# Moving expert gathers and six value tiles into an earlier stage of a fused decoder block, with a one-matmul gate scatter

## The chip, the cores and the metric

The kernel runs on one NeuronCore of a Trainium2 chip. The metric is the device time of one execution in microseconds (us); lower is better. Engines are named PE (TensorE; PEld is its weight loads), DVE (VectorE), ACT (ScalarE), POOL (GpSimd) and SP (SyncE, which here only issues DMAs).

## The reference

One decoder layer on 256 tokens of width 1024, fp32. Two gated attention mixers feed a merge, and the second half is a product-key expert layer (PEER). Only that half is touched:

```python
def peer_ffn(h, w_q, sub_k1, sub_k2, expert_u, expert_v):
    q = (ht @ w_q).reshape(T, 8, 256)
    s1, s2 = q[..., :128] . sub_k1, q[..., 128:] . sub_k2      # 128 keys each
    v1, i1 = top_k(s1, 16);  v2, i2 = top_k(s2, 16)
    vals, pos = top_k(v1 + v2 over all 256 pairs, 16)          # per token and head
    experts = i1[...] * 128 + i2[...];  gates = softmax(vals)
    a = einsum('cd,chkd->chk', x, expert_u[experts])
    return einsum('chk,chkd->cd', gelu(a) * gates, expert_v[experts])
```

Each token has 8 heads x 16 = 128 experts out of 16,384, and an expert is one row of 1024 floats in `expert_u` and one in `expert_v`.

## The kernel before, in words

The first 289 us compute the mixers, the merge, the second norm and the queries. What follows is the expert layer, in three stages that this document calls R, U and V.

**Two ways to the same sum.** The last 160 tokens (`ND`) go through all 16,384 experts densely. For each of 128 u tiles (128 experts x 1024, 512 KB from HBM), `u_tile` (L585) does eight fp32 matmuls of 160 columns into a PSUM bank, applies gelu, and leaves the activations in `ga`. In stage V, each of 128 v tiles is multiplied with `ga` by eight more such matmuls into four accumulators `acc` (L855). The first 96 tokens (`NG`, as sets of 64 and 32) use gathers: 96 indirect DMAs fetch 128 rows of u each (512 KB) into a tile `grow`, DVE takes the dot products (L622); 96 more fetch rows of v, which DVE scales and adds into `accG` (L633).

**Stage R** (u tiles 0 to 59): beside the u tiles, DVE finds the experts of all tokens (`retrieval`), in four pieces. Each piece decodes positions to indices with bf16 one-hots (L715) that are multiplied with a table, fp32 before (L717). `route` transposes indices and gates on PE (`ps_tri`, L751) into `eTb` and `gT`. The exponentials of a piece are summed on DVE (`se`, L729) before `tri` and these transposes.

**Stage U** (u tiles 60 to 127): the gates have to be put into `ga`, a zero nearly everywhere. `gate_group` (L802) does it for four tokens at a time, 40 times: DVE builds the one-hots `o2` and `o1` of both index halves (L811, L812), ACT multiplies `o1` by the gate (`og`, L814), DVE by the gate's rounding remainder (L815), and PE multiplies the one-hots, two f16 matmuls of 128 columns a token (L819). DVE and ACT multiply the result into `ga`.

**Stage V** (v tiles 0 to 127): the matmuls of L855, the remaining gathers, and for each v tile a `mark`: DVE copies one column of the loaded tile (L857).

**What sets the order.** Tile loads are issued by SP in program order into nine buffers (three tags with three buffers each), so that load i waits for the readers of tile i-9: PE, and in V also the mark. Gathers are issued by POOL, two at a time after every second gather's use, into two buffers of two slots: gathers n+3 and n+4 are issued when gather n (odd) has been read. `gather_steps(rate)` (L642) puts the uses into the program: `STEPS_R`, `STEPS_U` and `STEPS_V` are gathers per tile in R, U and V. Every engine works strictly in its own program's order.

**The end.** After the last v tile the accumulators are copied to `accT`, PE folds `accG` over its partitions (L865) and transposes `accT` on top (L872), DVE adds the residual `x1` (L875), and four DMAs write the output.

```python
STEPS_R, STEPS_U, STEPS_V = 0.55, 0.8, 0.9
...
if n % 2 == 1:                     # after the use of gather n
    for m in (n + 3, n + 4):
        fetch(m)
```

Of the kernel before, what the change touches and what calls it, by code (L numbers as in the profile page):

```python
# [39 lines left out]
STEPS_R = 0.55  # L40
STEPS_U = 0.8
STEPS_V = 0.9
GT = 4
# [27 lines left out]
def block_kernel(ctx: ExitStack, tc, x, g2, consts, small, wqkv, wkv5, wmg, w1kv, wup, wout, wq, uT, u, v, folds, out):  # L71
# [487 lines left out]
    gTb = ep.tile([P, 2, S], F16, name="gTb")  # L559
# [91 lines left out]
    with ExitStack() as ts:  # L651
# [8 lines left out]
        def retrieval(h, hg, tri):  # L660
# [14 lines left out]
            idf = sp.tile([P, 2, QH, TOPK], F32, name="idf")  # L675
            nc.vector.tensor_copy(idf, idx)
# [30 lines left out]
            diff = sp.tile([P, QH, TOPK], F32, name="diff")  # L707
            nc.vector.tensor_copy(diff[:, :, 0:1], idf[:, 0, :, 0:1])
            nc.vector.tensor_sub(diff[:, :, 1:], idf[:, 0, :, 1:], idf[:, 0, :, :TOPK - 1])
            hs = slice(QH * hg, QH * hg + QH)  # L710
            for w, (pos, op, table) in enumerate(((pa, ALU.is_ge, diff), (pb, ALU.is_equal, idf[:, 1]))):
                posb = sp.tile([P, QH, TOPK], BF16, name="posb")
                nc.vector.tensor_copy(posb.rearrange("p h j -> p (h j)"), pos)
                oh = sp.tile([P, QH, TOPK, TOPK], BF16, name="oh", tag="oh")
                nc.vector.tensor_tensor(oh, posb.unsqueeze(2).to_broadcast([P, QH, TOPK, TOPK]),  # L715
                                        steps16[:, w].unsqueeze(1).to_broadcast([P, QH, TOPK, TOPK]), op=op)
                nc.vector.tensor_mul(oh, oh, table.unsqueeze(3).to_broadcast([P, QH, TOPK, TOPK]))  # L717
                o2 = sp.tile([P, QH, TOPK // 2, TOPK], BF16, name="oh2", tag="oh2")
# [28 lines left out]
        def route(h, tri):  # L747
            with tc.issue_after(state["pe"].ins):
                pt = bank("ps_tri", "g")[:, :3 * P].rearrange("p (i t) -> p i t", t=P)
                for i in range(3):  # L750
                    nc.tensor.transpose(pt[:, i, :], tri[:, i].rearrange("p h j -> p (h j)"), C("ident"))  # L751
            nc.vector.tensor_copy(eTb[:, :, h * P:(h + 1) * P], pt[:, 0:2])
            r = slice(h * P, (h + 1) * P)
            nc.vector.tensor_copy(gTb[:, 0, r], pt[:, 2])
            nc.vector.tensor_copy(gT[:, r], gTb[:, 0, r])
            nc.vector.tensor_sub(gTb[:, 1, r], pt[:, 2], gT[:, r])
# [73 lines left out]

    groups = ND // GT
    done = 0
    for i in range(TOPK_TILES, NKEY):
# [7 lines left out]
        gather_steps(STEPS_U)  # L841

# [26 lines left out]
    for j in range(2):
        for h in (1, 0):  # L870
            for c in range(4):
                nc.tensor.matmul(fin[h][j][:, c * P:(c + 1) * P], accT[:, 4 * j + c, h * P:(h + 1) * P], cident,  # L872
                                 start=h == 1 and c == 0, stop=c == 3, skip_group_check=True)
            o = x1[:, h, j * 512:(j + 1) * 512]
            nc.vector.tensor_add(o, fin[h][j], o)  # L875
            nc.sync.dma_start(out[h, :, j * 512:(j + 1) * 512], o)
# [113 lines left out]
```

## Time and profile before

| | us |
|---|---|
| median of 3 runs | 942.36 (941.22 to 951.69) |
| the profiled execution's own time | 938.46 |
| its span in the profile | 936.7 |
| PE busy | 900.6 (96%) |
| DVE busy | 614.3 (66%) |
| ACT busy | 309.6 (33%) |
| POOL busy | 218.4 (23%) |
| mean granted TensorE clock | 0.999 of full |

The span is the time from the first to the last instruction of the program; the execution's own time has the launch around it. Stage R lasts from 289.3 to 425.7 us, U from 425.7 to 611.2, V from 611.2 to 925.4, and the end to 936.7. A busy share is an average over stages with different limits, so it is read by stage. An fp32 matmul of the program is recorded as two matmuls in the trace, a bf16 or f16 one as one.

### The profile page before, as it was taken

To read this page: it belongs to the slowest core of one execution; us is meant where nothing else is said; L and a number is where in the kernel's file an instruction comes from. 1 tells how busy PE (TensorE), PEld (TensorE's weight loads), DVE (VectorE), ACT (ScalarE), POOL (GpSimd) and SP (SyncE) were. 2 spreads that over 40 slices of the span, in tenths; PEclk is the share of its full clock that TensorE was granted. 3 is DMA by queue.
4 is the path that set the end of the run, shared out by engine and by line. 5 is a ranking of instruction groups with operands and counts; after the bars stand their busy time and mean duration, and the time that the engine had idled before them with its cause. 6 is when DMAs were issued, how large, how long until landed. Compare 5 with 4: busy or idle time off the path is not lost.

```text
span 936.7 us, 17034 instructions
## 1 busy us (share of the span) xinstructions
PE 900.6 (96%) x6433; PEld 842.9 (90%) x6433; DVE 614.3 (66%) x1663; ACT 309.6 (33%) x768; POOL 218.4 (23%) x213
## 2 busy tenths in 40 slices
PE   8999999999999999999999999999989989998987
PEld 6778867998899999999999999999988888988986
DVE  5886876577567689997778788644445544444444
ACT  6766776545541221326555455300000000000000
POOL 2000000000100223233232233333344333443330
PEclk9999999999999999999999999999999999999999
DMA  7665401556556999999999999999999999999994
GB/s 242 191 213 190 159 1 47 183 185 210 169 173 235 331 392 365 376 373 328 350 334 352 354 339 347 354 378 403 357 369 399 400 380 403 385 392 401 400 398 185
DMA packets 79570, 281.96 MB, mean 301 GB/s; under 512 B 10176, under 2 KB 10432, under 8 KB 79488
## 3 DMA queue, kind: packets, MB, share of 16 engines
q1 hardware_dynamic: 51088, 177.63, 52.6%
q0 software_dynamic: 28400, 103.25, 29.2%
q8 instruction: 51, 0.84, 0.3%
q14 instruction: 31, 0.25, 0.1%
HBM read 278.64 MB, written 1.05 MB: 299 GB/s over the span
## 4 chain that ended last, share of the span: by engine, by line
PE 56%; DMA 28%; issue 7%; POOL 3%; DVE 3%; ACT 2%; DVEq 0%; POOLq 0%; ACTq 0%; SPq 0%
PE ps_u L588 28%; DMA grow<-in_v_dram,gidx 21%; PE ps_g L819 4%; POOL grow L611 3%; DMA grow<-in_u_dram,gidx 3%; PE ps_q L121 2%; PE ps_mg L124 2%; PE ps_mg L121 2%; PE ps_q L124 2%; PE ps_q L122 2%; PE ps_mg L122 2%; PE ps_s L410 2%; PE ps_proj L171 1%; PE ps_pt L427 1%; DVE wlo L106 1%
## 5 line engine op out<-in xcount | busy, mean ns | idle before, releaser
L855 PE MATMUL acc<-ga,uvraw 128*128 128x160 f32 x2048 | 292.9, 302 | 21.3 <-DMA uvraw<-in_v_dram 19.5
L855 PEld LDWEIGHTS acc<-ga,uvraw 128*128 128x128 f32 x2048 | 279.9, 190 | 34.2 <-DMA uvraw<-in_v_dram 32.3
L588 PE MATMUL ps_u<-h2f,uvraw 128*128 128x160 f32 x2048 | 287.3, 299 | 0.0
L588 PEld LDWEIGHTS ps_u<-h2f,uvraw 128*128 128x128 f32 x2048 | 280.7, 190 | 0.1
L633 DVE SCALAR_TENSOR_TENSOR accG<-grow,gwt,accG 128x1024 f32<-128x1024 f32 x94 | 120.8, 1285 | 137.0 <-DMA grow<-in_v_dram,gidx 136.9
L611 POOL DMA_INDIRECT grow<-in_u_dram,gidx x96 | 102.1, 1063 | 302.2 <-DVE gdot L622 149.1
L611 POOL DMA_INDIRECT grow<-in_v_dram,gidx x96 | 106.0, 1104 | 166.0 <-DVE mark L857 150.0
L622 DVE CUSTOM_DVE_ANT_0 grow<-grow,h2d 128x1024 f32<-128x1024 f32 x96 | 116.7, 1218 | 34.6 <-DMA grow<-in_u_dram,gidx 34.5
L106 DVE TENSOR_TENSOR wlo<-wraw,whi 128x1024 fp32r<-128x1024 f32 (+1 forms) x80 | 95.5, 1196 | 37.1 <-ACT whi L105 37.0
L105 ACT CAST whi<-wraw 128x1024 fp32r<-128x1024 f32 (+1 forms) x80 | 82.0, 1029 | 65.5 <-PE ps_q L122 13.9
L868 ACT COPY accT<-acc 128x320 f32<-128x320 f32 x2 | 0.9, 426 | 270.9 <-PE acc L855 270.9
L592 ACT ACTIVATE ga<-ps_u 128x160 f32<-128x160 f32 (+32 forms) x124 | 33.5, 271 | 143.7 <-PE ps_u L588 143.4
L814 ACT ACTIVATE og<-o,gT 128x128 f16<-128x128 f16 x160 | 61.9, 568 | 15.9 <-PE ps_g L819 14.5
L819 PE MATMUL ps_g<-og,o 128*128 128x128 f16 x320 | 44.4, 294 | 0.0
L819 PEld LDWEIGHTS <-o 128*128 128x128 f16 x320 | 36.3, 116 | 1.5
L168 PE MATMUL ps_proj<-whi,hhi 128*128 128x512 f32 (+1 forms) x96 | 36.3, 381 | 1.3 <-ACT hhi L205 1.0
L489 POOL DMA_DIRECT2D gain<-in_g_dram x1 | 0.5, 533 | 151.2 <-DVE wlo L106 151.2
L169 PE MATMUL ps_proj<-whi,hlo 128*128 128x512 f32 (+1 forms) x96 | 35.7, 378 | 0.0
L121 PE MATMUL ps_mg<-hhi,whi 128*128 128x256 f32 x128 | 32.3, 288 | 0.0
L596 DVE TENSOR_TENSOR ga<-ga,au 128x160 f32<-128x160 f32 (+32 forms) x68 | 16.8, 247 | 23.4 <-ACT au L595 22.9
L122 PE MATMUL ps_mg<-hlo,whi 128*128 128x256 f32 x128 | 31.9, 285 | 0.0
L121 PE MATMUL ps_q<-h2hi,whi 128*128 128x256 f32 x128 | 31.7, 285 | 0.2 <-ACT h2hi L105 0.2
(256 smaller groups left out, 1126.0 us busy)
## 6 DMA issues: line engine op xcount, KB each, us to landing
uvraw<-in_uT_dram SPq DMA_DIRECT2D x128, 512.0 KB, 6.8
uvraw<-in_v_dram SPq DMA_DIRECT2D x128, 512.0 KB, 7.2
wraw<-in_wqkv_dram SPq DMA_DIRECT2D x20, 512.0 KB, 4.7
wraw<-in_wmg_dram SPq DMA_DIRECT2D x16, 512.0 KB, 3.6
wraw<-in_wq_dram SPq DMA_DIRECT2D x16, 512.0 KB, 4.3
wraw<-in_w1kv_dram SPq DMA_DIRECT2D x8, 512.0 KB, 4.0
wraw<-in_wup_dram SPq DMA_DIRECT2D x8, 512.0 KB, 3.6
wraw<-in_wout_dram SPq DMA_DIRECT2D x8, 512.0 KB, 4.5
```

Source lines behind the costliest of these rows:

```text
L105: nc.scalar.copy(hi, src)
L106: state["dve"] = nc.vector.tensor_sub(lo, src, hi)
L121: nc.tensor.matmul(ps, lh, rh, start=i == 0, stop=False)
L122: nc.tensor.matmul(ps, ll if lo_last else lh, rh if lo_last else rl, start=False, stop=False)
L124: nc.tensor.matmul(ps, lh if lo_last else ll, rl if lo_last else rh, start=False, stop=i == NC - 1)
L588: state["pe"] = nc.tensor.matmul(ps, raw[:, c * P:(c + 1) * P], h2f[:, c, NG:], start=c == 0, stop=c == NC - 1)
L611: nc.gpsimd.indirect_dma_start(out=dst, out_offset=None, in_=src, in_offset=bass.IndirectOffsetOnAxis(ap=gidx[:, j:j + 1], axis=0))
L622: nc.vector.tensor_tensor_reduce(out=g, in0=g, in1=h2d[k], scale=1.0, scalar=0.0, op0=ALU.mult, op1=ALU.add, accum_out=gdot[:, j:j + 1])
L633: nc.vector.scalar_tensor_tensor(accG[:, k], g, gwt[:, j:j + 1], accG[:, k], op0=ALU.mult, op1=ALU.add)
L814: nc.scalar.activation(og[0][:, :, k], o1[:, :, k], AF.Copy, scale=gT[:, t0 + k:t0 + k + 1])
L819: nc.tensor.matmul(ps[:, k, :], o2[:, :, k], og[i][:, :, k], start=i == 0, stop=i == 1, skip_group_check=True)
L855: nc.tensor.matmul(acc[c // 2][:, c % 2, 0:ND], raw[:, c * P:(c + 1) * P], ga_at(i), start=i == 0 and c % 2 == 0, stop=i == NKEY - 1, skip ...
```

## The change

- The gate scatter takes one fp32 matmul a token in place of two f16 ones: `o2` and `og` become fp32, the remainder's DVE product and the split tables `gTb` go.
- The decode tables (`diff`, and the second half of the indices, `idb`) become bf16.
- `STEPS_R` goes from 0.55 to 0.6 and `STEPS_U` from 0.8 to 1.0; `STEPS_V` stays.
- Six v tiles are fetched in U into a pool of their own (`first_v`), one every eighth u tile.
- Each mark is put behind the DVE instruction that `state["dve"]` names.
- The last two v tiles are worked accumulator by accumulator (bank by bank), and each bank's fold, transposes, add and output DMA (256 columns of both halves) are done in turn, alternately from SP and ACT.

```diff
-STEPS_R = 0.55
-STEPS_U = 0.8
+STEPS_R = 0.6
+STEPS_U = 1.0
 STEPS_V = 0.9
+FIRST_V = 6
+LAST = 2
...
-    def load_raw(src, i):
-        raw = wp.tile([P, DM], F32, name="uvraw", tag=("wraw", "whi", "wlo")[i % 3])
-        nc.sync.dma_start(raw, src[i])
+    def load_raw(src, i, home=None):
+        tag = f"first{i}" if home else ("wraw", "whi", "wlo")[i % 3]
+        raw = (home or wp).tile([P, DM], F32, name="uvraw", tag=tag)
+        state["sp"] = nc.sync.dma_start(raw, src[i])
...
-            idf = sp.tile([P, 2, QH, TOPK], F32, name="idf")
-            nc.vector.tensor_copy(idf, idx)
+            idf = sp.tile([P, QH, TOPK], F32, name="idf")
+            nc.vector.tensor_copy(idf, idx[:, 0])
+            idb = sp.tile([P, QH, TOPK], BF16, name="idb")
+            nc.vector.tensor_copy(idb, idx[:, 1])
...
-            diff = sp.tile([P, QH, TOPK], F32, name="diff")
+            diff = sp.tile([P, QH, TOPK], BF16, name="diff")
...
-            nc.vector.tensor_copy(gTb[:, 0, r], pt[:, 2])
-            nc.vector.tensor_copy(gT[:, r], gTb[:, 0, r])
-            nc.vector.tensor_sub(gTb[:, 1, r], pt[:, 2], gT[:, r])
+            nc.vector.tensor_copy(gT[:, r], pt[:, 2])
...
-        o2 = op.tile([P, P, n], F16, name="o2")
+        o2 = op.tile([P, P, n], F32, name="o2")
         o1 = op.tile([P, P, n], F16, name="o1")
-        og = [op.tile([P, P, n], F16, name=f"og{i}") for i in range(2)]
+        og = op.tile([P, P, n], F32, name="og")
...
-            nc.scalar.activation(og[0][:, :, k], o1[:, :, k], AF.Copy, scale=gT[:, t0 + k:t0 + k + 1])
-        nc.vector.tensor_mul(og[1], o1, rows(gTb[:, 1]))
+            nc.scalar.activation(og[:, :, k], o1[:, :, k], AF.Copy, scale=gT[:, t0 + k:t0 + k + 1])
         ps = bank("ps_g", "g").rearrange("p (t i) -> p t i", i=P)
         for k in range(n):
-            for i in range(2):
-                nc.tensor.matmul(ps[:, k, :], o2[:, :, k], og[i][:, :, k], start=i == 0, stop=i == 1,
-                                 skip_group_check=True)
+            nc.tensor.matmul(ps[:, k, :], o2[:, :, k], og[:, :, k], start=True, stop=True, skip_group_check=True)
...
+    first_v = pool(ctx, "first_v", 1)
+    early = []
...
         gather_steps(STEPS_U)
+        if i % 8 == 0 and i >= TOPK_TILES + 8 and len(early) < FIRST_V:
+            with tc.issue_after(state["sp"].ins):
+                early.append(load_raw(v, len(early), first_v))
...
-        state["dve"] = nc.vector.tensor_copy(mark, raw[:, 0:1])
-        gather_steps(STEPS_V if i < NKEY - 4 else 2 * NG)
+        with tc.issue_after(state["dve"].ins):
+            state["dve"] = nc.vector.tensor_copy(mark, raw[:, 0:1])
+        gather_steps(STEPS_V if i < NKEY - 5 else 2 * NG)
...
+    def finish(q):
+        r = slice(q * 256, (q + 1) * 256)
         for k in range(len(SETS)):
+            nc.tensor.matmul(fin[q][:, 0], fold[:, k], accG[:, k, r], start=k == 0, stop=False, skip_group_check=True)
+        for h in range(NH):
+            for c in range(2):
+                nc.tensor.matmul(fin[q][:, h, c * P:(c + 1) * P], accT[:, 2 * q + c, h * P:(h + 1) * P], cident,
+                                 start=False, stop=c == 1, skip_group_check=True)
+        nc.vector.tensor_add(x1[:, :, r], fin[q], x1[:, :, r])
+        (nc.scalar if q % 2 else nc.sync).dma_start(outr[:, :, r], x1[:, :, r])
+
     for q in range(4):
+        for c in (2 * q, 2 * q + 1):
+            for i in range(LAST):
+                state["pe"] = nc.tensor.matmul(acc[q][:, c % 2, 0:ND], raws[i][:, c * P:(c + 1) * P],
+                                               ga_at(NKEY - LAST + i), start=False, stop=i == LAST - 1,
+                                               skip_group_check=True)
         (nc.scalar.copy if q % 2 else nc.vector.tensor_copy)(accT[:, 2 * q:2 * q + 2, NG:], acc[q][:, :, 0:ND])
+        if q:
+            with tc.issue_after(state["pe"].ins):
+                finish(q - 1)
+    finish(3)
```

How the change moves instructions, at two places on DVE (the number behind a name tells buffers apart). The first is the end of R, where the last piece's `se` and `tri` precede the transposes that open U; the `L622` and `L624` rows with `grow` are each the use of one gather. Before:

```order
L722 TENSOR_TENSOR tri_3068<-oh2_4648 128x64
L622 ISA grow_4481,gdot_2760<-grow_4481,h2d0_2514 128x1024
...
L622 ISA grow_4590,gdot_2760<-grow_4590,h2d0_2514 128x1024
...
L622 ISA grow_4590,gdot_2760<-grow_4590,h2d0_2514 128x1024
...
L729 TENSOR_REDUCE se_4684<-ex_4681 128x4
L730 RECIPROCAL se_4684<-se_4684 128x4
L731 SCALAR_TENSOR_TENSOR tri_3068<-ex_4681,se_4684 128x64
L752 CAST eTb_2752<-ps_tri_4713 128x2x128
```

and of the change:

```order
L726 TENSOR_TENSOR tri_3067<-oh2_4658 128x64
L624 ISA grow_4513,gdot_2759<-grow_4513,h2d0_2514 128x1024
...
L624 ISA grow_4600,gdot_2759<-grow_4600,h2d0_2514 128x1024
...
L624 ISA grow_4600,gdot_2759<-grow_4600,h2d0_2514 128x1024
...
L624 ISA grow_4664,gdot_2759<-grow_4664,h2d0_2514 128x1024
...
L733 TENSOR_REDUCE se_4694<-ex_4691 128x4
L734 RECIPROCAL se_4694<-se_4694 128x4
L735 SCALAR_TENSOR_TENSOR tri_3067<-ex_4691,se_4694 128x64
```

Before, three uses stood between the last index piece and `se`, the 26th to the 28th of all; now there are four, the 28th to the 31st. The 28th is the second of its buffer, the 31st the first of the buffer that is fetched when the 28th has been read.

The second is the turn from U to V (`ga<-ga,au` is a late u tile's product, `mark` belongs to a v tile). Before:

```order
L596 TENSOR_TENSOR ga_1_4741<-ga_1_4741,au_6674 128x152
L622 ISA grow_6524,gdot_2760<-grow_6524,h2d0_2514 128x1024
...
L826 SCALAR_TENSOR_TENSOR ga_0_2765<-ps_g_6692,ga_0_2765 128x60x4
L826 SCALAR_TENSOR_TENSOR ga_1_4741<-ps_g_6692,ga_1_4741 128x62x4
L857 COPY mark_6833<-uvraw_6834 128x1
L596 TENSOR_TENSOR ga_1_4741<-ga_1_4741,au_6716 128x156
L622 ISA grow_6620,gdot_2760<-grow_6620,h2d0_2514 128x1024
...
L857 COPY mark_6833<-uvraw_6836 128x1
L857 COPY mark_6833<-uvraw_6847 128x1
L596 TENSOR_TENSOR ga_1_4741<-ga_1_4741,au_6732 128x156
```

and of the change:

```order
L598 TENSOR_TENSOR ga_1_4750<-ga_1_4750,au_6640 128x160
L635 SCALAR_TENSOR_TENSOR accG_2760<-grow_6595,gwt_2758,accG_2760 128x1024
L866 COPY mark_6653<-uvraw_5125 128x1
L635 SCALAR_TENSOR_TENSOR accG_2760<-grow_6595,gwt_2758,accG_2760 128x1024
L866 COPY mark_6653<-uvraw_5354 128x1
L866 COPY mark_6653<-uvraw_5581 128x1
L635 SCALAR_TENSOR_TENSOR accG_2760<-grow_6628,gwt_2758,accG_2760 128x1024
L866 COPY mark_6653<-uvraw_5810 128x1
L866 COPY mark_6653<-uvraw_6037 128x1
```

Before, the first marks stood among U's last products, and 78 gather uses (of 192) came ahead of the first mark; now all of U's products come first, with 99 uses. The last use stands behind mark 122 before and behind mark 104 now, and 22 marks follow it without one. Up to the sixteenth mark there are 94 uses before and 110 now. Ahead of the first gate one-hot of U there are 28 before and 31 now. On SP, the six early v loads stand singly among the u loads, the last of them 14 u loads ahead of the other 122.

## Rows read from the trace of the kernel before

**Rows 1.** The page, part 4: the chain that ended last, by engine and line.

```profile
PE 56%; DMA 28%; issue 7%; POOL 3%; DVE 3%; ACT 2%; DVEq 0%; POOLq 0%; ACTq 0%; SPq 0%
```

**Rows 2.** Windows: stretch, us; PE, PEld, DVE, ACT, POOL busy; clock, DMA share, GB/s.

```profile
289.30:425.70 136.40, 136.40 (x1015) 136.31 (x1014) 115.40 (x536) 34.72 (x82) 34.33 (x32) 1.00 0.92 349
425.70:611.20 185.50, 185.50 (x1409) 183.98 (x1408) 140.43 (x379) 93.63 (x335) 54.67 (x52) 1.00 0.95 345
611.20:660.00 48.80, 48.80 (x362) 48.80 (x361) 21.92 (x48) 0.52 (x2) 18.50 (x18) 1.00 1.00 392
660.00:925.40 265.40, 244.07 (x1692) 231.17 (x1691) 128.97 (x204) 0.43 (x1) 101.29 (x92) 1.00 0.99 385
```

**Rows 3.** The chain in order of time: start us, us, what.

```profile
355.98 26.08 PE ps_u L588 x192
...
429.10 0.94 PE ps_g L819 x8
...
928.89 3.59 PE fin L872 x32
```

**Rows 4.** Waits of SP's queue in V: total us, times, longest.

```profile
SPq L582 <- DVE mark L857: 233.9, 95, 5.4
```

**Rows 5.** Waits of DVE for gathers, in V and in U.

```profile
DVE accG L633 <- DMA grow<-in_v_dram,gidx: 136.9, 93, 3.7
...
DVE grow L622 <- DMA grow<-in_u_dram,gidx: 10.1, 10, 1.9
```

**Rows 6.** The uses of v gathers: ns min/median/max, first and last start us.

```profile
L633 DVE SCALAR_TENSOR_TENSOR accG<-grow,gwt,accG x94: 1283/1285/1346, 657.7 to 922.6; 128x1024 f32<-128x1024 f32 x94
```

**Rows 7.** DMA issues, 430 to 600 us: what, count, median us to landing.

```profile
uvraw<-in_v_dram SPq DMA_DIRECT2D x4, 512.0 KB, 5.0
...
grow<-in_u_dram,gidx POOLq DMA_INDIRECT x50, 7.8
```

**Rows 8.** Timeline at the turn from R to U.

```profile
418.53 1.22 DVE L622 CUSTOM_DVE_ANT_0 grow<-grow,h2d 128x1024 f32<-128x1024 f32 x1
...
420.02 1.68 POOL L611 DMA_INDIRECT grow<-in_u_dram,gidx  x1 [8.10 <-DVE gdot L622]
...
421.96 0.21 DVE L729 TENSOR_REDUCE se<-ex 128x4 f32<-128x64 f32 x1
...
423.13 0.49 PE L751 MATMUL ps_tri<-cst,tri 128*128 128x128 f32 x3
```

**Rows 9.** Groups by form: busy us, mean ns, idle before.

```profile
L622 DVE CUSTOM_DVE_ANT_0 grow<-grow,h2d 128x1024 f32<-128x1024 f32 x96 | 116.7, 1218 | 34.6 <-DMA grow<-in_u_dram,gidx 34.5
...
L819 PEld LDWEIGHTS <-o 128*128 128x128 f16 x320 | 36.3, 116 | 1.5
...
L815 DVE TENSOR_TENSOR og<-o,gTb 128x512 f16<-128x512 f16 x40 | 16.7, 417 | 0.0
L811 DVE TENSOR_TENSOR o<-iob,eTb 128x512 f16<-128x512 f16 x40 | 16.6, 415 | 0.0
...
L715 DVE TENSOR_TENSOR oh<-posb,steps 128x1024 bf16<-128x1024 bf16 x8 | 5.5, 688 | 0.1
L717 DVE TENSOR_TENSOR oh<-oh,diff 128x1024 bf16<-128x1024 bf16 x4 | 4.9, 1225 | 0.0
...
L245 DVE TENSOR_TENSOR q_h<-q_h,sml 128x512 f32<-128x512 f32 x6 | 4.0, 684 | 0.0
L872 PEld LDWEIGHTS fin<-cident,accT 128*128 128x128 f32 x32 | 3.7, 192 | 0.5 <-issue 0.5
```

**Rows 10.** Eight stretches of 25 us in V: the slowest and the fastest.

```profile
750.00:775.00 25.00, 21.94 (x152) 20.56 (x151) 10.95 (x17) 0.00 (x0) 8.50 (x9) 1.00 0.99 375
...
850.00:875.00 25.00, 22.71 (x158) 21.66 (x159) 12.29 (x19) 0.00 (x0) 10.15 (x9) 1.00 1.02 405
```

**Rows 11.** Busy time by stretch: the last 2.2 us, behind the last matmul.

```profile
934.50:936.70 2.20, 0.00 (x0) 0.00 (x0) 0.00 (x0) 0.00 (x0) 0.00 (x0) 0.57 0.12 44
```

**Rows 12.** Timeline: the opening matmuls of the program.

```profile
1.24 3.59 PE L192 MATMUL ps_heat<-heat 128*128 128x512 bf16 x8 [1.24 <-DVE heat L189]
```

More of the change, by code (lines that the diff above doesn't have):

```diff
@@ L558, in block_kernel @@
     gT = ep.tile([P, S], F32, name="gT")
-    gTb = ep.tile([P, 2, S], F16, name="gTb")
     dp = pool(ctx, "dots", 2)
@@ L706, in retrieval @@
             yield 1.6
-            diff = sp.tile([P, QH, TOPK], F32, name="diff")
-            nc.vector.tensor_copy(diff[:, :, 0:1], idf[:, 0, :, 0:1])
-            nc.vector.tensor_sub(diff[:, :, 1:], idf[:, 0, :, 1:], idf[:, 0, :, :TOPK - 1])
+            diff = sp.tile([P, QH, TOPK], BF16, name="diff")
+            nc.vector.tensor_copy(diff[:, :, 0:1], idf[:, :, 0:1])
+            nc.vector.tensor_sub(diff[:, :, 1:], idf[:, :, 1:], idf[:, :, :TOPK - 1])
             hs = slice(QH * hg, QH * hg + QH)
-            for w, (pos, op, table) in enumerate(((pa, ALU.is_ge, diff), (pb, ALU.is_equal, idf[:, 1]))):
+            for w, (pos, op, table) in enumerate(((pa, ALU.is_ge, diff), (pb, ALU.is_equal, idb))):
                 posb = sp.tile([P, QH, TOPK], BF16, name="posb")
@@ L848, in block_kernel, with v_load @@
     mark = dp.tile([P, 1], F32, name="mark", bufs=1)
-    ahead = []
-    for i in range(NKEY):
+    ahead = early
+    def v_load(i):
         while len(ahead) <= AHEAD and i + len(ahead) < NKEY:
             ahead.append(load_raw(v, i + len(ahead)))
-        raw = ahead.pop(0)
+        return ahead.pop(0)
+    for i in range(NKEY - LAST):
+        raw = v_load(i)
         for c in range(NC):
             nc.tensor.matmul(acc[c // 2][:, c % 2, 0:ND], raw[:, c * P:(c + 1) * P], ga_at(i),
-                             start=i == 0 and c % 2 == 0, stop=i == NKEY - 1, skip_group_check=True)
-        state["dve"] = nc.vector.tensor_copy(mark, raw[:, 0:1])
-        gather_steps(STEPS_V if i < NKEY - 4 else 2 * NG)
+                             start=i == 0 and c % 2 == 0, stop=False, skip_group_check=True)
+        with tc.issue_after(state["dve"].ins):
+            state["dve"] = nc.vector.tensor_copy(mark, raw[:, 0:1])
+        gather_steps(STEPS_V if i < NKEY - 5 else 2 * NG)
     accT = hpool.tile([P, NC, S], F32, name="accT", tag="h2f")
@@ L861, in block_kernel @@
     psum.append(psd)
-    fin = [[bank("fin", "u", 3) for j in range(2)], [bank("fin", "u", 3), bank("fin1", "g")]]
-    for j in range(2):
-        for k in range(len(SETS)):
-            nc.tensor.matmul(fin[0][j], fold[:, k], accG[:, k, j * 512:(j + 1) * 512], start=k == 0, stop=False,
-                             skip_group_check=True)
-    for q in range(4):
-        (nc.scalar.copy if q % 2 else nc.vector.tensor_copy)(accT[:, 2 * q:2 * q + 2, NG:], acc[q][:, :, 0:ND])
[L869 to L876, printed above, removed]
+    raws = [v_load(i) for i in range(NKEY - LAST, NKEY)]
@@ new lines, in block_kernel @@
+    outr = out.rearrange("h p d -> p h d")
+    fin = [bank("fin", "u", 3).rearrange("p (h d) -> p h d", h=NH) for _ in range(3)]
+    fin.append(bank("fin3", "g").rearrange("p (h d) -> p h d", h=NH))
+    def finish(q):
+        r = slice(q * 256, (q + 1) * 256)
+        for k in range(len(SETS)):
+            nc.tensor.matmul(fin[q][:, 0], fold[:, k], accG[:, k, r], start=k == 0, stop=False, skip_group_check=True)
[5 more added lines that the diff above has]
+        (nc.scalar if q % 2 else nc.sync).dma_start(outr[:, :, r], x1[:, :, r])
```

## Prediction

> **What bounds the kernel now.** I read the chain of waits first, by engine and then in order of time, then busy time by stretch, then the waits of the engines that the chain passes through.
>
> The chain is PE for 56% and DMA for 28% of the span [rows 1]. In R and U, PE is busy without a gap (136.40 of 136.40 us, 185.50 of 185.50) [rows 2], so there only PE work counts, and whatever makes PE wait. In V it is not: after 660 us PE is busy 244.07 of 265.40 us, with the DMA share at 0.99 and 385 GB/s, and the stretch before it at 1.00 and 392.
>
> One u or v tile is 16 recorded matmuls, and 192 of them took 26.08 us [rows 3]: 26.08/12 = 2.173 us a tile, so 128 v tiles are 278.2 us of PE work. V lasts 314.2 us (611.2 to 925.4). **36 us of V is waiting**, the largest loss there is. The gate groups are 40 x 0.94 = 37.6 us [rows 3], and 68 x 2.173 + 37.6 = 185.4 us is the whole of U.
>
> In V, SP waits 233.9 us for marks [rows 4], and DVE, whose work the marks are, waits 136.9 us for gathered rows [rows 5]. The gathers are used from 657.7 to 922.6 us, 94 of them, so one in 264.9/93 = 2.85 us, though a use takes 1.285 [rows 6]. V is therefore a loop: the next load waits for a mark, the mark stands behind a gather, the gather waits for a DMA that shares its rate with the loads. Bytes settle it: by their issues 112 gathers and 119 loads of 0.524 MB fall into V, 121.1 MB, which at 385 to 392 GB/s is V's length.
>
> In U, DVE waits only 10.1 us for gathers [rows 5], and the DMA moves 345 GB/s at a share of 0.95 [rows 2].
>
> **The change, part by part.** The profiled execution took 938.46 us, 3.9 us below the median of 942.36; the sum is against 938.46, and 3.9 is added at its end.
>
> *Gate matmul.* A group was eight f16 matmuls in 0.94 us. It becomes four fp32 ones, recorded as eight. The fold's last step, 32 records of the same fp32 shape, took 3.59 us [rows 3], 0.224 us a matmul; four are 0.90. That is 0.04 x 40 = **-1.7 us**, all on PE's path, and U needs 183.8. The upper bound is that the fp32 weight loads, 192 ns each against 116 in f16 [rows 9], are not hidden: 8 x 0.192 = 1.54 a group, +24 us. I take the first, because those 32 records also had loads of 192 ns and still came every 112 ns. Nothing below -1.7 is to be had, as the columns stay.
>
> [...]
>
> *DVE in U.* L815 goes (-16.7 us), `o2` in fp32 costs 684 in place of 415 ns by the nearest fp32 row of that size (+10.7), and the higher rates bring some 14 more uses of about 1.3 us (+17.7) [rows 6, 9]. 140.4 becomes 152 of some 185 us [rows 2]: the cover holds, and this costs nothing.
>
> *bf16 tables.* L717 took 1225 ns and may come down to L715's 688 [rows 9], or not at all, as its table is still read with a step of zero: 0 to 4.3 us of DVE, all beside PE, except at the next point.
>
> *The turn from R to U.* PE must have the last transposes, these need `tri`, and `tri` stands on DVE behind the gather uses. Before, DVE began the three at 418.53 and the sum `se` at 421.96, and PE began the transposes at 423.13, with no gap [rows 8]. Now four uses stand there, and the row of the fourth (the 31st) is issued only after the 28th has been read. DVE reaches the 28th some 2.6 us later for the two more gathers of R and up to 3.2 earlier for bf16: I take 420. It is read by 421.2, the issue follows 0.4 later (as POOL's at 420.02 follows the use begun at 418.53 [rows 8]), the row lands 7.8 us after that by the gathers' median [rows 7], 429.4, and is read by 430.7; `se`, `tri` and PE's start follow 1.2 later, as before. The transposes begin at 431.9 instead of 423.1: PE idles **+8 us** (with the next one-hots as late). With the 5.0 us of a v tile's landing in place of 7.8 [rows 7] and an early DVE it would be 4. [...] So 4 to 11.
>
> *U's own transfers.* Now 68 u tiles, 68 gathers and six v tiles: 142 x 0.524 = 74.4 MB. To fit into 183.8 us they need 405 GB/s. Stretches of 25 us in V had 375 to 405 [rows 10]; at 388 it takes 191.9, and at V's pace of 2.85 us a gather 193.8. Nine buffers, filled while PE idles at the turn, absorb a part. I take 188, **+2.5 us** over 185.5 with the matmul's gain in it (-1.7 to +8).
>
> *V.* About 93 gathers and 98 loads remain until the last use: 191 x 0.524 = 100.1 MB, 258 us at 388, some 5 until the last row has landed and is read, then 15 tiles of PE at 2.173, 32.6 (22 marks follow the last use, and I let PE stand seven tiles ahead of DVE there): 296 against 314.2, **-18 us**. At the old pace, 93 x 2.85 = 265 with the same 5 and 32.6 behind it, 303, it is -11; at 405 GB/s throughout -29.
>
> *The end.* The folds and transposes are the same columns and the last add and output are of the same size: 0. At worst the two last tiles wait together for the last load, +2.2.
>
> The sum: +8 + 2.5 - 18 = -7.5, so 931 for an execution like the profiled one, and with 3.9 **935 us**.
>
> **The rivals.**
>
> *B, no hold at the turn.* DVE comes to the 28th gather so early, or the 31st lands so fast, that PE has its transposes in time. For it: DVE waited little in U [rows 5] and bf16 may save up to 4.3 us. Against it: a landing had to fit into the three uses of 3.7 us [rows 8]. Then -15.5: 927.
>
> *C, U becomes the stretch that the DMA sets, slower.* U's 345 GB/s stood at a share of 0.95 [rows 2]; if that is its ceiling, 345/0.95 = 363, or 345 itself if u gathers can't be served faster, 74.4 MB take 205 to 216 us, 20 to 30 more than U did. DVE, waiting for gathers, would then hand PE its one-hots late. With +8 and -18 the middle is +15: 957. It turns on U's rate: at 381 GB/s, 195 us, the kernel is where it was. Against it: in U SP waited for no mark and PE never for a load, so the rate was asked for, not limited, and V reaches 375 to 405 on the same queues.
>
> [...]
>
> *D, the fp32 weight loads are not hidden*: +24, 960, against the 112 ns pace above.
>
> *E, V keeps its pace.* Each gather waits for the one two before it, and if that, not bytes, is the 2.85 us, V gains 11 and not 18: 942. For it: DVE waits 93 times for gathers [rows 5]. Against it: the DMA share of 0.99.
>
> **How the numbers follow.** The forecast, 935, has 0.37; B 0.24; E 0.18; C 0.15; D 0.03; 0.03 is for what I don't see. The forecast's own spread is 927 to 944, from the bounds of the turn (4 to 11) and of U and V. A range from 920 to 951 takes in the forecast, E and most of B, and leaves out C, D and B's lower end: 0.2. A change under 1%, 9.4 us, can't be told from none here. Faster (below 933) holds most of B and 0.4 of the forecast, 0.37; slower (above 951.8) most of C, D and a part of what I don't see, 0.18; 0.45 lies between.
>
> **What would show it.** The transposes near 432 us, with PE idle some 8 us ahead of them and DVE waiting for one u gather, show the hold; none there is B. U at 183 to 188 us of work and 390 GB/s or more shows step four; a U of 205 at 363 is C. Groups of 0.90 us settle D. V near 296 us, with PE without a gap in its last 15 to 20 tiles and gathers used faster than one in 2.75 us, shows the V step; 2.85 is E. The prediction is wrong outright if V's length hardly moves, since then neither bytes nor marks set it.

## The result, and the profile after

The changed kernel took 981.98 us (median of 4 runs, 980.9 to 986.49) against 944.13 for the kernel before: a ratio of 1.040, interval [1.033, 1.047]. **It is 4% slower; 935 was forecast.** The profiled execution took 981.82 us, its span is 979.7.

Stretches of the changed kernel, columns as in [rows 2]: the turn from R to U, U, and V up to the last gather use.

```profile
423.60:431.90 8.30, 1.96 (x15) 1.72 (x14) 3.12 (x9) 1.21 (x3) 3.81 (x4) 0.79 0.96 356
...
432.00:661.60 229.60, 229.60 (x1425) 229.60 (x1426) 158.51 (x365) 87.78 (x337) 69.00 (x66) 0.99 0.89 318
661.60:926.60 265.00, 248.40 (x1746) 238.08 (x1744) 127.46 (x198) 0.30 (x1) 98.98 (x93) 1.00 0.99 380
```

U is 230 us long with PE busy all the time, at fewer GB/s than before: PE simply has more to do there. What, the chain in order of time tells (start us, us, what):

```profile
432.43 3.59 PE ps_u L590 x16
440.28 1.95 PE ps_g L819 x8
442.23 4.35 PE ps_u L590 x32
...
926.91 37.21 PE acc L863 x272
964.12 2.17 PE acc L890 x16
```

A gate group takes **1.95 us where it took 0.94** [rows 3]; a u tile still takes 4.35/2. The last two rows matter later: 17 tiles and the two of the end run on PE behind the last gather use. The groups by form (columns as in [rows 9]):

```profile
L819 PE MATMUL ps_g<-og,o 128*128 128x128 f32 x320 | 84.7, 421 | 0.0
L819 PEld LDWEIGHTS ps_g<-og,o 128*128 128x128 f32 x320 | 78.3, 329 | 0.0
...
L813 DVE TENSOR_TENSOR o<-iob,eTb 128x512 f32<-128x512 f16 x40 | 27.2, 681 | 0.0
...
L719 DVE TENSOR_TENSOR oh<-posb,steps 128x1024 bf16<-128x1024 bf16 x8 | 5.5, 686 | 0.1
L721 DVE TENSOR_TENSOR oh<-oh,diff 128x1024 bf16<-128x1024 bf16 x4 | 4.9, 1225 | 0.0
...
L882 PEld LDWEIGHTS fin<-cident,accT 128*128 128x128 f32 x32 | 4.2, 192 | 0.2
```

A weight load of the gate takes 329 ns on average; one of the same type and size at the end takes 192. The bf16 table (L721) takes the 1225 ns that it took in fp32, so that part gained nothing. The turn, from the timeline (start us, us, engine, line):

```profile
421.44 1.22 DVE L624 CUSTOM_DVE_ANT_0 grow<-grow,h2d 128x1024 f32<-128x1024 f32 x1
...
422.93 1.68 POOL L613 DMA_INDIRECT grow<-in_u_dram,gidx  x1 [8.09 <-DMA uvraw<-in_uT_dram]
...
430.06 1.23 DVE L624 CUSTOM_DVE_ANT_0 grow<-grow,h2d 128x1024 f32<-128x1024 f32 x1 [5.11 <-DMA grow<-in_u_dram,gidx]
...
431.21 0.22 DVE L733 TENSOR_REDUCE se<-ex 128x4 f32<-128x64 f32 x1
...
431.96 0.48 PE L755 MATMUL ps_tri<-cst,tri 128*128 128x128 f32 x1 [6.40 <-DVE tri L735]
```

The 28th gather is read at 421.44, the 31st issued at 422.93, DVE waits 5.11 us for it, and PE idles 6.40 us; in 8.3 us around that the clock averages 0.79, and the tile behind it takes 3.59 us instead of 2.17. Last, the waits that answer to [rows 4, 5] and the uses that answer to [rows 6]:

```profile
SPq L584 <- DVE mark L866: 207.5, 82, 10.2
```

```profile
DVE accG L635 <- DMA grow<-in_v_dram,gidx: 132.8, 87, 4.6
...
DVE grow L624 <- DMA grow<-in_u_dram,gidx: 10.4, 8, 5.1
```

```profile
L635 DVE SCALAR_TENSOR_TENSOR accG<-grow,gwt,accG x94: 1274/1284/1351, 660.3 to 926.6; 128x1024 f32<-128x1024 f32 x94
```

V's uses come one in 266.3/93 = 2.86 us, as before (2.85).

The stages of all kernels, from the profiled execution of each (U: from the last of the transposes to the first v matmul; V: from there to the span's end). One of the seven runs of e4_f16_gate took 3154.83 us against 947 to 954 for the others; the median of 950.41 has it in, without it the median is 949.55, and the ratio given for e4 leaves it out.

| kernel | median us | PE idle at the turn | U | V and end |
|---|---|---|---|---|
| before | 944.13 | 0 | 187.9 | 325.5 |
| the change | 981.98 | 6.4 | 229.7 | 318.0 |
| e1_og_flat | 977.17 | 7.1 | 225.5 | 317.4 |
| e2_o2_flat | 977.55 | 7.0 | 224.4 | 316.8 |
| e3_both_flat | 952.20 | 7.5 | 195.2 | 321.4 |
| e13_pairs | 950.79 | 8.3 | 193.7 | 320.5 |
| e4_f16_gate | 950.41 | 7.3 | 192.9 | 319.5 |
| e5_third_pair | 924.91 | 0.3 | 188.1 | 309.1 |
| e6_steps_v | 923.46 | 7.6 | 194.9 | 293.7 |
| e7_steps_r | 946.26 | 0 | 196.6 | 328.0 |
| e8_spread | 925.81 | 0 | 187.9 | 311.0 |
| e9_third_steps_v | 912.26 | 0.3 | 187.9 | 295.6 |
| e10_third_flat | 911.32 | 0.3 | 186.4 | 296.6 |
| e14_third_pairs | 913.44 | 0.3 | 188.0 | 297.0 |
| e12_no_early | 915.29 | 0.3 | 187.9 | 299.0 |
| e11_before_third | 933.96 | 0 | 187.9 | 320.1 |

Each ratio below is to runs of the kernel before that were made beside the kernel in question; their medians lie between 941.29 and 944.13 us.

For the change, the 43.0 us between the two spans are 2.1 ahead of R (its clock was 0.97 in the first 50 us of that execution), 6.6 at the turn, **41.8 in U** and -7.5 in V and the end.

### The profile page after: what moved, and what is told of

The parts are those of the page before. It is cut to its first block, busy times and chain, and to the rows that moved or that the text cites. A ratio compares the mean times of both kernels' runs of the same rounds, so it can differ in the third digit from the quotient of the medians.

```text
span 979.7 us, 17012 instructions
## 1 busy us (share of the span) xinstructions
PE 940.4 (96%) x6441; PEld 888.1 (91%) x6441; DVE 616.0 (63%) x1621; ACT 303.0 (31%) x768; POOL 213.0 (22%) x213
## 3 DMA queue, kind: packets, MB, share of 16 engines
HBM read 278.64 MB, written 1.05 MB: 285 GB/s over the span
## 4 chain that ended last, share of the span: by engine, by line
PE 61%; DMA 26%; issue 4%; DVE 3%; POOL 2%; ACT 2%; SPq 0%; DVEq 0%; ACTq 0%; POOLq 0%
PE ps_u L590 27%; DMA grow<-in_v_dram,gidx 20%; PE ps_g L819 8%; PE acc L863 4%; POOL grow L613 2%; DMA wraw<-in_wqkv_dram 2%; PE ps_q L123 2%; PE ps_mg L126 2%; PE ps_mg L123 2%; PE ps_q L126 2%; PE ps_q L124 2%; PE ps_mg L124 2%; PE ps_s L412 1%; PE ps_pt L429 1%; PE ps_proj L173 1%
## 5 line engine op out<-in xcount | busy, mean ns | idle before, releaser
L863 PE MATMUL acc<-ga,uvraw 128*128 128x160 f32 x2016 | 285.6, 301 | 16.9 <-DMA uvraw<-in_v_dram 15.7
L863 PEld LDWEIGHTS acc<-ga,uvraw 128*128 128x128 f32 x2016 | 275.1, 190 | 27.2 <-DMA uvraw<-in_v_dram 26.2
L590 PEld LDWEIGHTS ps_u<-h2f,uvraw 128*128 128x128 f32 x2048 | 286.0, 192 | 0.0
L613 POOL DMA_INDIRECT grow<-in_u_dram,gidx x96 | 99.8, 1040 | 303.8 <-DVE gdot L624 157.6
L613 POOL DMA_INDIRECT grow<-in_v_dram,gidx x96 | 102.9, 1072 | 170.5 <-DVE mark L866 134.0
L624 DVE CUSTOM_DVE_ANT_0 grow<-grow,h2d 128x1024 f32<-128x1024 f32 x96 | 116.6, 1217 | 10.4 <-DMA grow<-in_u_dram,gidx 10.4
L819 PE MATMUL ps_g<-og,o 128*128 128x128 f32 x320 | 84.7, 421 | 0.0
L819 PEld LDWEIGHTS ps_g<-og,o 128*128 128x128 f32 x320 | 78.3, 329 | 0.0
L816 ACT ACTIVATE og<-o,gT 128x128 f32<-128x128 f16 x160 | 57.5, 512 | 66.4 <-PE ps_g L819 58.0
```

What stands on the lines that cost most here:

```text
L590: state["pe"] = nc.tensor.matmul(ps, raw[:, c * P:(c + 1) * P], h2f[:, c, NG:], start=c == 0, stop=c == NC - 1)
L613: nc.gpsimd.indirect_dma_start(out=dst, out_offset=None, in_=src, in_offset=bass.IndirectOffsetOnAxis(ap=gidx[:, j:j + 1], axis=0))
L624: nc.vector.tensor_tensor_reduce(out=g, in0=g, in1=h2d[k], scale=1.0, scalar=0.0, op0=ALU.mult, op1=ALU.add, accum_out=gdot[:, j:j + 1])
L816: nc.scalar.activation(og[:, :, k], o1[:, :, k], AF.Copy, scale=gT[:, t0 + k:t0 + k + 1])
L819: nc.tensor.matmul(ps[:, k, :], o2[:, :, k], og[:, :, k], start=True, stop=True, skip_group_check=True)
```

## The experiments

### Why the gate matmul costs twice

`o2` and `og` hold four tokens interleaved, so that one token's values are four elements apart: 8 bytes in f16 before, 16 in fp32 now.

**e1_og_flat**, the moving operand contiguous:

```diff
-        og = op.tile([P, P, n], F32, name="og")
+        og = op.tile([P, n, P], F32, name="og")
...
-            nc.tensor.matmul(ps[:, k, :], o2[:, :, k], og[:, :, k], ...)
+            nc.tensor.matmul(ps[:, k, :], o2[:, :, k], og[:, k, :], ...)
```

> The changed kernel with one edit: og, the moving operand of the gate matmul, is laid out with each token's 128 values next to each other (before: one in four, a step of 16 bytes); o2, the weights, keeps the step. A gate group of the changed kernel takes 1.94 us (0.243 a record). Theory M (the fp32 moving operand is read slowly with a step): groups of 0.90 us, 40 x 1.04 = 42 us less PE work, 982 down to about 940 to 947. Theory W (the fp32 weights are loaded slowly with a step): no change, 1.94 us and 982. Theory F (fp32 weight loads of 128 columns are slow however they lie): no change either, 982.

**e2_o2_flat**, the weights contiguous:

```diff
-        o2 = op.tile([P, P, n], F32, name="o2")
+        o2 = op.tile([P, n, P], F32, name="o2")
...
-        nc.vector.tensor_tensor(o2, iob, rows(eTb[:, 1]), op=ALU.is_equal)
+        nc.vector.tensor_tensor(o2.rearrange("p t i -> p i t"), iob, rows(eTb[:, 1]), op=ALU.is_equal)
...
-            nc.tensor.matmul(ps[:, k, :], o2[:, :, k], og[:, :, k], ...)
+            nc.tensor.matmul(ps[:, k, :], o2[:, k, :], og[:, :, k], ...)
```

> The changed kernel with one edit: o2, the weights of the gate matmul, is laid out with each token's 128 values next to each other (DVE writes it with a step of 512 bytes instead); og keeps its step of 16 bytes. Theory M (moving operand): no change, groups of 1.94 us, 982. Theory W (strided fp32 weights): groups of 0.90 us, 940 to 947. Theory F (fp32 loads whatever the layout): 1.94 us, 982. If DVE's o2 takes over 2 us with the wide step (0.68 now), its 40 add over 50 us to DVE in U and U is set by DVE: U over 200 us whatever PE does.

**e3_both_flat**, both edits:

> The changed kernel with both edits: o2 and og are contiguous for each token. Theories M and W: groups of 0.90 us, as the fp32 matmuls of the same shape at the end (3.59 us for 32 records); 40 x 1.04 = 42 us off PE in U: 940 where PE sets U, 947 if U is then set by its 74 MB at some 385 GB/s. Theory F: 1.94 us and 982. If M and W each hold a part, this run shows 0.90 and the two single edits lie between.

Measured: 977.17, 977.55 and 952.20 us (ratios to before 1.034 [1.030, 1.039], 1.038 [1.034, 1.042], 1.011 [1.006, 1.016]). A gate group in the chain of e1, and its weight loads:

```profile
446.86 1.84 PE ps_g L819 x8
```

```profile
L819 PEld LDWEIGHTS ps_g<-og,o 128*128 128x128 f32 x320 | 77.9, 327 | 0.0
```

the same of e2:

```profile
445.52 1.81 PE ps_g L819 x8
```

```profile
L819 PEld LDWEIGHTS ps_g<-og,o 128*128 128x128 f32 x320 | 62.7, 203 | 4.5
```

and of e3, with `o2` on DVE:

```profile
562.57 0.89 PE ps_g L819 x8
```

```profile
L813 DVE TENSOR_TENSOR o<-iob,eTb 128x512 f32<-128x512 f16 x40 | 42.0, 1051 | 0.0
L819 PEld LDWEIGHTS ps_g<-og,o 128*128 128x128 f32 x320 | 39.9, 191 | 7.6 <-ACT au L597 7.1 <-issue 0.2 <-ACT og L816 0.2
```

Neither M nor W fell out as put: each alone leaves the group at 1.8, and only both together give 0.89, the price that I had forecast. Either operand with the step is enough to hold the group, and the loads tell the two apart: with the step in the weights alone (e1) they take 327 ns, with the step in the moving operand alone (e2) 203, near the contiguous 191, and the group is as slow. So the slow loads are one half of the cause and the moving operand is the other. F falls: e3's contiguous fp32 loads of 191 ns are hidden. The last fence shows the layout's own price, `o2` in 1.05 us instead of 0.68 on DVE; PE waits 6.1 us for it in that profile, and 952 is 5 us above the upper end expected.

**e13_pairs**, fp32 values of a token 8 bytes apart:

```diff
-        o2 = op.tile([P, P, n], F32, name="o2")
+        o2 = op.tile([P, 2, P, 2], F32, name="o2")
...
-        og = op.tile([P, P, n], F32, name="og")
+        og = op.tile([P, 2, P, 2], F32, name="og")
...
-            nc.tensor.matmul(ps[:, k, :], o2[:, :, k], og[:, :, k], ...)
+            nc.tensor.matmul(ps[:, k, :], o2[:, k // 2, :, k % 2], og[:, k // 2, :, k % 2], ...)
```

> The changed kernel with one edit: o2 and og hold the four tokens as two pairs, so that a token's fp32 values lie 8 bytes apart (16 in the changed kernel, 4 in e3). Theory L (what costs is that no two of the elements read share 16 bytes): groups of 0.9 us, as in e3, and with a cheaper o2 on DVE (below e3's 1.05 us) U at or below e3's 195 us: about 950. Theory S (any step between fp32 elements costs): groups of 1.4 to 1.8 us, 965 to 978.

950.79 us, 1.007 [1.003, 1.010]; U 193.7. The gate's weight loads and `o2` by form, and a group in the chain of e14_third_pairs, which has the same layout:

```profile
L820 PEld LDWEIGHTS ps_g<-og,o 128*128 128x128 f32 x320 | 41.8, 197 | 2.7 <-ACT au L597 2.0 <-ACT ga L594 0.2 <-ACT og L817 0.2
...
L813 DVE TENSOR_TENSOR o<-iob,eTb 128x512 f32<-128x512 f16 x40 | 27.2, 681 | 0.0
```

```profile
450.71 0.94 PE ps_g L823 x8
```

The runs fit theory L: a step of 8 bytes costs 6% (0.94 against 0.89), one of 16 bytes 120%. S, by which any step costs, is out. Steps between 8 and 16 bytes and other types were not run, so that what counts is the sharing of 16 bytes is the theory's part and not measured.

### What is left without the gate

**e4_f16_gate**: the two f16 matmuls, the remainder product and `gTb` of before put back, everything else of the change kept.

> The changed kernel with the gate of before: two f16 matmuls a token with f16 one-hots and the remainder's product on DVE, everything else of the change kept. If the gate is the whole of the loss in U: groups of 0.94 us, U 40 us shorter, 982 to 942 to 949 (the upper end if U's transfers set it). If the rest of the change costs by itself, the time stays above 950. The idle of PE at the turn from R to U stays at 6 to 8 us, and V stays at 324 us with the end.

950.41 us, 1.008 [1.005, 1.011]: the gate is some 32 us of the loss, and the rest of the change still loses 0.8%. Its stretches, U and V up to the last use:

```profile
432.70:625.60 192.90, 191.03 (x1425) 187.83 (x1426) 153.90 (x404) 87.55 (x337) 68.33 (x65) 0.99 0.97 373
625.60:891.90 266.30, 248.69 (x1746) 238.06 (x1744) 129.69 (x203) 0.30 (x1) 101.32 (x95) 1.00 1.00 381
```

That is just above the 942 to 949 of the first theory, and V is no shorter than in the change. The next four start from e4.

**e5_third_pair**, six gathers under way:

```diff
-FIRST_V = 6
+FIRST_V = 4
...
-        for n in range(4):
+        for n in range(6):
             fetch(n)
...
-                for m in (n + 3, n + 4):
+                for m in (n + 5, n + 6):
```

(and a third buffer of two slots; the smaller `FIRST_V` makes room for it, and no run separates the two)

> The change with the f16 gate (e4_f16_gate, 950) and a third gather buffer of two slots, so that six gathers are under way and gather n+5 is issued when n (odd) has been read; FIRST_V is 4 instead of 6 for the room it takes. In e4 V's gathers are used one in 2.77 us and the DMA share is 1.0 at 380 to 396 GB/s. Theory C (the chain of gathers sets V's pace: four slots and some 8 us of landing): the pace falls to 2.2 or less and V with the end from 319.5 to below 305. Theory B (bytes set it): the rate and the pace stay, V within 4 us of 319.5. By both the hold at the turn from R to U goes, since the row of the 31st gather is issued two uses earlier: PE's idle there from 7.3 to under 2 us. So C: about 928; B: about 943.

**e6_steps_v**:

```diff
-STEPS_V = 0.9
+STEPS_V = 0.77
```

> The change with the f16 gate and STEPS_V 0.77 instead of 0.9: the last gather use stands behind mark 121 instead of 104, so the v loads of the last 19 tiles share the stretch with gathers instead of running alone. My reading of why V gained only 6 us of the 18 forecast: the 96 gathers of V come at one in 2.8 us as before, PE waits all that time, and behind the last one 19 tiles follow at PE's own 2.17 us with the DMA half idle. If so, V with the end is set by its 215 transfers (112.7 MB at 386 GB/s, 292 us, and 11 for the end): 303 instead of 319.5, 950 to about 934; if the chain of gathers and not bytes set the pace, V can fall to 290, 921. Rival (V is bound by something else, the marks or the tile buffers): no change, 950.

e5 takes 924.91 us (0.983 [0.979, 0.987]), e6 923.46 (0.981 [0.976, 0.985]). U and V up to the last use, of e5:

```profile
425.80:611.60 185.80, 185.80 (x1410) 184.27 (x1410) 155.30 (x401) 94.56 (x337) 69.75 (x67) 1.00 1.01 392
611.60:853.00 241.40, 235.04 (x1639) 223.63 (x1638) 129.24 (x199) 0.30 (x1) 118.83 (x91) 1.00 1.03 407
```

of e6:

```profile
433.10:628.10 195.00, 191.06 (x1426) 187.74 (x1427) 154.51 (x405) 87.84 (x337) 69.36 (x65) 0.99 0.97 370
628.10:904.60 276.50, 276.06 (x2013) 273.63 (x2013) 132.23 (x218) 0.30 (x1) 97.98 (x95) 1.00 1.01 398
```

and the uses of e5's v gathers:

```profile
L639 DVE SCALAR_TENSOR_TENSOR accG<-grow,gwt,accG x94: 1275/1284/1339, 610.3 to 853.0; 128x1024 f32<-128x1024 f32 x94
```

e5: the hold at the turn is gone (0.3 us), U is PE's own work again (busy 185.8 of 185.8) though it now moves 392 GB/s, and V's gathers come one in 242.7/93 = 2.61 us at 407 GB/s, where e4's 381 had stood at a DMA share of 1.00. So neither B nor C as put: the four slots did hold V back (V falls by 10.4, not by 4 or less), but the pace stopped at 2.61, above the 2.2 of C, with the DMA at 407, near the 406 to 409 of the other kernels with six gathers under way. e6: with the same four slots, spreading the uses alone makes V PE's own (276.06 of 276.50 us busy), 293.7 us with the end, 25.8 less than e4. That is less than the 303 that its bytes take at 386 GB/s: it moved 398. The gain that I had forecast for V was there, but the program left it lying in the last 19 tiles.

**e7_steps_r** (`STEPS_R = 0.55` again):

> The change with the f16 gate and STEPS_R 0.55 as before the change, so that 28 gather uses and not 31 stand ahead of the last sum of exponentials. If the wait for the 31st gather is what holds PE at the turn from R to U (7.3 us of idle PE in e4, and the first u tile behind it at the lower clock), the idle goes, the clock stays, and U starts some 9 us earlier; of these, three more gathers in V at 2.8 us may be given back: 950 to 941 to 949. Rival (the later DVE alone makes the hold): PE still idles over 4 us and the time stays at 950.

946.26 us, 1.006 [1.003, 1.009]. The idle at the turn is gone, as the first theory says; of the 7.3 us, V gives back 8.5 with three more gathers (328.0 against 319.5) in a profiled execution that was 6 us above the median. Between the medians the turn and the three gathers together are worth 3 to 4 us, with intervals that overlap: that the idle goes is shown, what it is worth in the end is not settled.

**e8_spread** (`STEPS_R` 0.55, `STEPS_U` 0.95, `STEPS_V` 0.8):

> The change with the f16 gate and its gathers spread so that no stretch is left without them: STEPS_R 0.55, STEPS_U 0.95, STEPS_V 0.8 (uses ahead of the turn 28, ahead of the first mark 93, the last behind mark 124). If the turn costs 9 us and V's empty last part 16, and U at 0.95 a tile stays at its present 193 us: 950 - 9 - 14 = about 927, faster than the kernel before (942). By bytes, U and V together are (68 + 128 + 164) x 0.524 = 188.7 MB, 489 us at 386 GB/s, 425 + 489 + 11 = 925. Rival (the early v tiles and higher U rate gain nothing over before): 940 or more.

925.81 us, 0.985 [0.979, 0.990]: as expected, and against e4 by rates alone.

### Together, and what the change is worth

**e9_third_steps_v** is e5 with `STEPS_V` 0.77, **e10_third_flat** the same with e3's gate, **e14_third_pairs** with e13's, **e12_no_early** is e9 with `FIRST_V` 0.

> e5_third_pair (925) with STEPS_V 0.77: f16 gate, six gathers under way, FIRST_V 4, the last gather use behind mark 121. In e5 the DMA ran at 409 GB/s until the gathers were used up at 853 us, and 30 tiles followed with the DMA idle for half; in e6 (four slots, 0.77) it ran at 408 throughout. If the two gains are of different kinds they add: no hold, U 188 us, V 216 transfers = 113 MB at 409, 277 us, at PE's own floor of 278, and 11 behind it: 423 + 188 + 290 = 901 in the profile, 903 to 907 as a time. Rival (both only lift the rate, and it can be lifted once): no better than e6 without its hold, 923 - 8 = 915 or more.

> As e9_third_steps_v, but with the one fp32 gate matmul a token and both operands contiguous (as in e3) in place of the two f16 ones. If PE sets U, groups of 0.89 us against 0.94 make 2 us less: 901 to 905. If DVE's o2 with its wide step (1.07 us, and no remainder product: 1.49 against 1.26 us a group, 9 us over U) delays PE, as PE waited some 6 us for DVE's o2 in e3: 5 to 8 us more than e9.

> As e10_third_flat (six gathers under way, STEPS_V 0.77, FIRST_V 4, one fp32 gate matmul), with the pair layout of e13. Theory L: the same groups of 0.89 us and 911, as DVE has room there either way. Theory S: groups of 1.4 us or more, 20 us more, 930 or above.

> e9_third_steps_v with FIRST_V 0: no v tile is fetched in U, everything else as in e9. If the early tiles matter (V is set by its bytes): four more loads of 0.524 MB in V at 409 GB/s, 5 us more than e9. If PE sets V there, no difference (within 2 us).

912.26, 911.32, 913.44 and 915.29 us (0.969 [0.965, 0.973], 0.967 [0.963, 0.971], 0.968 [0.962, 0.974], 0.972 [0.968, 0.976]): **3% faster than the kernel before**, whichever gate. That is 5 to 9 us above what I expected of e9, mostly in V: 295.6 where 290 was put. U in e10 is 1.5 us shorter than in e9, near what the forecast gave the single fp32 matmul (1.7). The early tiles are worth 3 us between the medians of e9 and e12, with intervals that overlap: not settled. Stretches of e9, U and V:

```profile
425.80:611.00 185.20, 185.20 (x1407) 183.61 (x1406) 155.15 (x404) 94.81 (x336) 70.85 (x68) 1.00 1.01 394
611.00:890.00 279.00, 277.59 (x2015) 273.90 (x2014) 134.17 (x223) 0.61 (x2) 106.50 (x91) 1.00 1.00 396
```

PE is busy in all of U and in 277.6 of 279 us of V, where 126 tiles at 2.173 would be 273.8: from the turn on little is left but PE's own work.

**e11_before_third**, the kernel before with the third buffer alone:

> The kernel before with one edit: the third gather buffer of two slots, six gathers under way. Its rates (0.55, 0.8, 0.9) and its gate stay, its last use stands behind mark 122. If the pace of V in the kernel before was set by its four slots, not by what the DMA can move, the DMA goes from 386 to some 408 GB/s and V from 314 to about 297 us (121.1 MB): 942 to about 924. Then the change's own moves (higher rates, early v tiles) are worth what e9 lies below it. Rival (V of before was at the limit of the DMA): 942.

933.96 us, 0.990 [0.987, 0.993]. A miss by 10 us. Its V up to 915 us:

```profile
611.00:915.00 304.00, 294.54 (x2018) 275.93 (x2017) 156.01 (x261) 1.12 (x5) 138.13 (x109) 1.00 1.00 397
```

The mean rises from 386 to 397 GB/s only, as it takes in a slower beginning and end (340 GB/s from 607 to 630 us and 394 from 887 to 910, with 408 to 409 between them). From 640 to 840 us, the kernel before and e11 (bytes moved; issues of v tile loads, with the median us from issue to landing):

```profile
DMA packets 21220, 77.37 MB, mean 387 GB/s; under 512 B 2366, under 2 KB 2366, under 8 KB 21206
...
uvraw<-in_v_dram SPq DMA_DIRECT2D x75, 512.0 KB, 6.8
```

```profile
DMA packets 22403, 81.74 MB, mean 409 GB/s; under 512 B 2484, under 2 KB 2484, under 8 KB 22388
...
uvraw<-in_v_dram SPq DMA_DIRECT2D x81, 512.0 KB, 19.4
```

With six gathers under way a tile takes 19.4 us to land where it took 6.8, at 409 GB/s: transfers now queue for the DMA, and bytes set V, which they did not before. Between e11 and e9 lie 22 us. e5, which has the change's moving of gathers and v tiles into U at the old `STEPS_V`, stands 9 us below e11, and the 0.77 that fewer gathers in V then allow brings 13 more. U takes the moves at no cost to PE, 345 GB/s become 394. By bytes the sum fits: e9 moves 110.5 MB in V up to 890 us, e11 120.7 up to 915, and at 409 GB/s the difference is an estimated 25 us, as V's 24.5. The change's other parts (bf16 tables, marks, the end) go along in e5 and e9 without a run of their own.

## Why the prediction was wrong, step by step

**The gate matmul, the step that failed**: -1.7 us forecast, (1.95 - 0.94) x 40 = +40 measured, outside the bound of +24 as well. I took the price from the row that was nearest in type, columns and count, the end's 32 records [rows 3], and did not compare the operands' layout: those lie contiguous, the gate's lie 16 bytes apart. The bound (rival D) looked only at the weight load, as 192 ns; the load itself grew to 329, and the moving operand, which no rival named, holds the group by itself (e2). e3 gives 0.89 with the same instruction, so the row was right for its layout. Of the 50 us between the forecast sum of -7.5 and the 43.0 measured, U is 39. Between the change and e4 U gives back 36.8 of the 40 (229.7 and 192.9): PE is idle for 1.9 us of e4's U (191.0 of 192.9 busy). That the gathers are behind this, which in the change hide behind the longer PE work, is not shown by a run.

By layout a group took 0.94 us with a token's values 8 bytes apart (e13's layout, in e14), 1.81 and 1.84 at 16 bytes on one operand, 1.95 at 16 bytes on both, and 0.89 contiguous (e3). Why 16 bytes cost so much is not shown by a run. e3's 0.89 is less than its eight loads of 191 ns put end to end, 1.53 us, so contiguous fp32 loads don't set the group.

**DVE in U**: right for the change. `o2` took 681 ns (684 forecast), and DVE was busy 158.5 of 229.6 us (152 forecast), which PE did not feel. **bf16 tables**: 0 of 0 to 4.3 us; the lower end.

**The turn**: right in place and cause, near in size. Transposes were forecast at 431.9 and begun at 431.96, and that they agree so closely is luck: R itself began 2.1 us later, and from there DVE came to the 28th gather a little earlier and the 31st landed a little faster than forecast. So PE idled 6.4 us, not 8, and the clock's fall added 1.4 (3.59 against 2.17, at a granted clock of 0.61 from 432.43 to 436.02 us). The turn's upper bound, 11, has a price for a fallen clock in it that no run shows; 1.4 is what was measured in its place. e5 and e7 each take the cause away, in different ways, and the idle goes. Rival B is out.

**U's own transfers**: within the bounds, as e4 shows, where PE doesn't cover it: U +5.0 us with the clock's 1.4 in it, against +2.5 (-1.7 to +8). Rival C is out: U ran at 373 GB/s in e4 and 394 in e9, above the 363 that I had read off the share.

**V, the second step that failed**: -18 forecast, -7.5 measured, -6.0 in e4. The 12 us between -18 and -6.0 are about what e4 lies above 937, the forecast without the gate's gain. The tail was longer: 19 tiles followed the last use, not 15, 8.7 us, so PE stood three tiles ahead of DVE's marks and not seven. The stretch up to the last use came out as long as forecast (265.0 us against 258 + 5), but not for the reason given. I priced it by its bytes; what set it was rival E's loop, each gather waiting for an earlier one. In the chain of the change these landings follow one another (start us, us, what):

```profile
857.18 8.47 DMA grow<-in_v_dram,gidx
...
868.53 8.57 DMA grow<-in_v_dram,gidx
...
880.00 8.79 DMA grow<-in_v_dram,gidx
```

They start 11.4 us apart, one round through the four slots, which is 2.86 us a gather, as before the change. With two more slots the pace falls to 2.61 (e5), so the loop and not the bytes held it. The forecast counted the tail, but didn't ask what the rate 0.9 does with fewer gathers: it ends them at mark 104 and leaves the DMA at a share of 0.64 and 239 GB/s behind it (926.6 to 964.1 us). e6 shows what 0.77 makes of the same four slots: V is 31.8 us shorter than in the kernel before, more than I forecast.

**A DMA share of 0.99 as proof that bytes set V**: wrong. e5 moved 407 GB/s where e4 moved 381, both at a share of 1.00 or above; two more slots are the cause that the landings of e11 bear out.

**The end**: right. From the last of L863's matmuls, at 964.1, to the span's end are 15.6 us, of which two tiles are 4.35; the remaining 11.2 compare with 11.3 before.

## What to carry to other kernels

A price taken from another row holds only if the operands lie alike: compare type, size and the step between the elements that one instruction reads, for the weights and the moving operand both (here 0.89 us a group contiguous, 1.95 at 16 bytes). When work is moved out of a stretch, set that stretch's own rate again, or it ends early and leaves the resource idle behind it. A DMA share near one was no ceiling here (381 GB/s at 1.00 in e4, 407 at 1.03 in e5); what the same stretch moves with more requests under way, and how long one then takes to land, tells more.

## What the runs showed of the hardware

- The gate's fp32 matmuls with an operand at a step of 16 bytes ran at half pace: 1.81 us a group for the moving operand, 1.84 for the weights, 1.95 for both, 0.94 at 8 bytes, 0.89 contiguous. Weight loads took 327 to 329 ns at 16 bytes, 191 to 203 otherwise. The f16 gate's step of 8 bytes gave 0.94 with eight matmuls; it was not run contiguous.
- DVE wrote a fp32 128x512 tile in 681 ns contiguous or in pairs, and in 1047 to 1066 with a step of 512 bytes.
- A DVE product with a broadcast table took 1225 ns with the table in fp32 and in bf16.
- Around 6.4 us without a matmul the granted clock averaged 0.79 of full over 8.3 us, and the next 16 matmuls took 3.59 us against 2.17, at a granted clock of 0.61.
- One core moved 406 to 408 GB/s over 240 to 268 us of mixed gathers and tile loads (e5, e9, e12), at a share of 1.02 to 1.03. With four gathers under way a v tile landed 6.8 us after its issue at 387 GB/s, with six 19.4 us at 409 (the kernel before and e11, 640 to 840 us).
